# Five gate panels in seven half-size products each, with the gates kept in DRAM

## The chip, the core and the metric

The kernel runs on one core of a Trainium2 chip. The metric is the device time of one launch, in microseconds; lower is better. Matmuls run on TensorE (PE), element-wise work on VectorE (DVE) and ScalarE (ACT), and transfers are issued from the queues of SyncE (SP) and GpSimd (POOL).

## The reference, cut to what matters

One decoder layer over 1024 prompt tokens and 64 sample tokens, which the kernel handles together as TOK = 1088 columns. D_MODEL is 1024. The part that the change touches is this:

```python
u = rmsnorm(x)
a, q, k, v, g_a, g_b = split(u @ w_in)          # g_a and g_b are 1024 wide each
A = pooled(a) @ w_pa                            # 512 -> 1024
B = attention(q, k, v) @ w_pb                   # 256 -> 1024
h = x + (sigmoid(g_a) * A + sigmoid(g_b) * B) @ w_o
y = h + relu(rmsnorm(h) @ w_up)**2 @ w_down
```

## The kernel before, in words

Activations lie transposed in SBUF, features on the 128 partitions and the 1088 tokens along the free axis: `act[0][k]` and `act[1][k]` are the high and low part of feature block k (0 to 7). Every fp32 operand is split in two this way (`split`: ACT copies the high part, DVE subtracts it to get the low part), and every product takes three passes (high by high, high by low, low by high). A gemm over 8 feature blocks is thus 24 matmuls.

A weight panel is 1024 features by 256 outputs. `panel` loads it in pieces of 512 columns through a ring of three 256 KB buffers, tag `raw`, and splits each piece into one of three `places`. A raw buffer takes its next load only when ACT and DVE have both read it. Other things go through the same ring, among them the operands of the mix.

The order on PE is the order in which the code is written (a manual schedule). The order on the other engines and queues comes from the framework's scheduler; each engine then runs its own list strictly in turn.

The stages around the change, in order of time:

- Gates: eight panels, ga0 to ga3 and gb0 to gb3. `gate` computes one unit: one of three token chunks (384, 384, 320) by one of two output blocks m, 24 matmuls into one PSUM bank (`pga`, `pgb`), then a multiply on DVE with the norm `rb_g` and a sigmoid on ACT. The first two panels run among the last of the attention work.
- Mix: `branches` loads the pooled and the attention features through the raw ring and splits them into `ab`. For each panel d and unit, `pa` is 12 matmuls and `pb` 6; DVE multiplies them with the gates and adds. For d below 3 the result is split and stored to DRAM (`mix_d`), and brought back into `act` at the end by POOL transfers. Mix units alternate with units of gb on PE.
- w_o: four panels d, chunk by chunk, m = 0 then m = 1, each gemm into a bank of its own out of four (`acc_tile`, tile name `ph`). DVE adds the residual `xr` on the way out into `y` (line 1161).
- Up and down projections, with a scheme of seven half-size products (M1 to M7). Such a product is 24 matmuls of 272 columns into a `pair`, a PSUM tile of two banks, and `unit` runs the seven of them. `prep_up` forms and splits the sums of weight quarters.

## Time and profile before

| | us |
|---|---|
| median of 3 runs | 1484.96 (1481.98 to 1486.16) |
| profiled execution | 1481.76, of which the span of the trace is 1480.0 |
| PE busy | 1445.0 (98%) |
| DVE busy | 1011.0 (68%) |
| ACT busy | 686.6 (46%) |
| POOL busy | 411.3 (28%) |

Times within the trace are counted from the start of the span. The granted clock of PE averages 0.989 of full speed. In the stretches that the change touches, gates begin at 408.7 us, the mix ends at 681.98, w_o runs from there, and the first up product begins at 781.07.

### The profile page before, as it was taken

How to read it: one execution, taken by the hardware profiler on the slowest of the kernel's cores; microseconds unless marked ns; L12 is line 12 of the kernel's file. 1: busy time of each engine (PE TensorE's matmuls, PEld its weight loads, DVE VectorE, ACT ScalarE, POOL GpSimd, SP SyncE). 2: the span in 40 equal slices, each digit the busy share in tenths (PEclk: the TensorE clock that was granted, in tenths of full speed). 3: DMA queues.
4: the chain of work that ended last, by engine and by line, in shares of the span. 5: the costliest groups of instructions: out<-in, count | busy, mean ns of one | idle time of the engine just before them, and what ended most of it. 6: DMA issues, size and time to landing. Idle time of an engine off the chain costs nothing.

```text
span 1480.0 us, 28012 instructions
## 1 busy us (share of the span) xinstructions
PE 1445.0 (98%) x10595; PEld 1396.9 (94%) x10595; DVE 1011.0 (68%) x1949; ACT 686.6 (46%) x1885; POOL 411.3 (28%) x619
## 2 busy tenths in 40 slices
PE   8999899999999999999998999999999999999998
PEld 8988788878999999999998999999998999999998
DVE  7555555767864443434668989888987566777786
ACT  8566755567774222222345665655555322222220
POOL 1611246645400000010200121111225444544430
PEclk9999999999999999999999999999999999999999
DMA  6311766874445657478620767766768797567542
GB/s 218 97 47 63 194 144 169 210 185 116 125 140 178 221 167 255 163 205 285 249 101 25 288 263 265 277 249 250 258 256 312 294 365 305 228 269 279 218 186 113
DMA packets 124277, 304.72 MB, mean 206 GB/s; under 512 B 19111, under 2 KB 72045, under 8 KB 118830
## 3 DMA queue, kind: packets, MB, share of 16 engines
q1 hardware_dynamic: 102334, 192.27, 39.4%
q0 software_dynamic: 21376, 109.88, 20.4%
q8 instruction: 83, 1.36, 0.4%
q10 hardware_dynamic: 432, 0.79, 0.2%
q14 instruction: 52, 0.43, 0.1%
HBM read 218.49 MB, written 128.05 MB: 234 GB/s over the span
## 4 chain that ended last, share of the span: by engine, by line
PE 75%; issue 11%; DMA 5%; DVE 4%; POOL 3%; ACT 1%; SPq 0%; POOLq 0%; ACTq 0%; DVEq 0%
PE p1d L1199 12%; PE pga L136 6%; PE pgb L136 6%; PE ph L136 6%; PE pqk L136 6%; PE p2d L1199 6%; PE p1u L1199 5%; PE pv L136 4%; PE a L264 3%; PE pa L136 3%; PE p3d L1199 3%; PE p2u L1199 2%; POOL z_d L1332 2%; DMA raw_qkv<-in_w_in_dram 2%; DVE places L94 2%
## 5 line engine op out<-in xcount | busy, mean ns | idle before, releaser
L1199 PE MATMUL p1d<-act,places 128*128 128x272 f32 x1104 | 191.3, 288 | 3.2 <-DVE yd L1579 1.4
L1199 PEld LDWEIGHTS p1d<-act,places 128*128 128x128 f32 x1104 | 163.1, 188 | 4.7 <-DVE yd L1579 2.5
L1332 POOL DMA_DIRECT2D z_d<-zs_M x105 | 56.2, 536 | 244.4 <-DVE zs_M L94 241.2
L1629 POOL DMA_DIRECT2D out_kv_sample_dram<-in_cache_kv_dram x44 | 22.1, 504 | 318.4 <-ACT places L93 302.0
L1199 PE MATMUL p1u<-act,places 128*128 128x272 f32 x768 | 104.5, 293 | 5.2 <-DVE y L1161 3.9
L1579 DVE TENSOR_TENSOR yd<-yd,p1d 128x544 f32<-128x544 f32 x116 | 83.0, 716 | 38.6 <-PE p1d L1199 38.4
L1199 PEld LDWEIGHTS p1u<-act,places 128*128 128x128 f32 x768 | 100.9, 193 | 5.8 <-ACT act L1285 4.1
L93 ACT ACTIVATE places<-sd 128x512 fp32r<-128x512 f32 x64 | 37.4, 625 | 143.7 <-issue 106.9
L1199 PE MATMUL p1u<-t,places 128*128 128x272 f32 x768 | 101.5, 288 | 0.7 <-ACT q L1446 0.7
L1199 PEld LDWEIGHTS p1u<-t,places 128*128 128x128 f32 x768 | 98.2, 188 | 0.8 <-ACT q L1446 0.8
L136 PE MATMUL pga<-act,places 128*128 128x384 f32 (+1 forms) x576 | 98.0, 328 | 0.0
L136 PE MATMUL pgb<-act,places 128*128 128x384 f32 (+1 forms) x576 | 97.8, 326 | 0.0
L1199 PE MATMUL p2d<-act,places 128*128 128x272 f32 x528 | 94.0, 288 | 1.7 <-DVE places L94 1.0
L136 PEld LDWEIGHTS pgb<-act,places 128*128 128x128 f32 x576 | 95.4, 188 | 0.0
L136 PE MATMUL ph<-act,places 128*128 128x384 f32 (+2 forms) x624 | 95.4, 314 | 0.0
L136 PEld LDWEIGHTS ph<-act,places 128*128 128x128 f32 x624 | 95.3, 188 | 0.0
L136 PEld LDWEIGHTS pga<-act,places 128*128 128x128 f32 x576 | 94.6, 188 | 0.3
L93 ACT ACTIVATE places<-rd 128x512 fp32r<-128x512 f32 x64 | 37.1, 625 | 94.6 <-PE p1d L1199 94.6
L1199 PEld LDWEIGHTS p2d<-act,places 128*128 128x128 f32 x528 | 78.8, 188 | 2.3 <-DVE places L94 1.2
L561 POOL TENSOR_TENSOR mr<-ms,mhalf 128x4 f32<-128x4 f32 (+2 forms) x39 | 49.8, 1276 | 110.6 <-DVE ms L560 105.0
L1531 POOL TENSOR_TENSOR sd<-rd 128x128 f32<-128x128 f32 x64 | 38.5, 602 | 128.9 <-DVE places L94 115.0
L94 DVE TENSOR_TENSOR zs_M<-q,zs_M 128x544 fp32r<-128x544 f32 x75 | 54.0, 722 | 19.1 <-ACT zs_M L93 19.0
(383 smaller groups left out, 3674.0 us busy)
## 6 DMA issues: line engine op xcount, KB each, us to landing
z_d<-zs_M POOLq DMA_DIRECT2D x105, 544.0 KB, 4.6
act<-z_d SPq DMA_DIRECT2D x73, 544.0 KB
out_kv_sample_dram<-in_cache_kv_dram POOLq DMA_DIRECT2D x36, 960.0 KB, 7.4
ru<-in_w_up_dram SPq DMA_DIRECT2D x16, 1024.0 KB
rd<-in_w_down_dram SPq DMA_DIRECT2D x15, 1024.0 KB
raw_qkv<-in_w_in_dram SPq DMA_DIRECT2D x36, 256.0 KB
zc<-z_d SPq DMA_DIRECT2D x16, 544.0 KB
pck<-in_cache_kv_dram SPq DMA_DIRECT2D x32, 256.0 KB
```

The costliest lines, as they stand in the source:

```text
L93: ins = s_.activation(dst_hi, src, AF.Copy)
L94: v_.tensor_tensor(dst_lo, src, dst_hi.bitcast(F32), op=ALU.subtract)
L136: last_mm[0] = t_.matmul(out, lhs(a, k), rhs(b, k), start=(j == 0), stop=(j == len(terms) - 1))
L264: last_mm[0] = t_.matmul(pts[m][:, :n], wt[:, a, kk, m * P:(m + 1) * P], act4[b][kk][:, :, part4(c)], start=(p == 0 and kk == 0), stop=(p ...
L561: g_.tensor_tensor(r[:n, :H], ms[:n, :H], mhalf[:n, :H], op=ALU.pow)
L1199: last_mm[0] = t_.matmul(pt[:, s, :R4], w(a, k), z(b, k, s), start=(start and j == 0), stop=(j == len(terms) - 1), skip_group_check=True)
L1332: g_.dma_start(z_d[f][AT[m]], st.rearrange("p b l -> p (b l)").bitcast(F32))
L1531: ins = g_.tensor_tensor(s[:, 0], a21, a22, op=ALU.add)
L1579: v_.tensor_tensor(part, part, p[src], op=ALU.add)
L1629: ins = g_.dma_start(d, a)
```

## The change

Panels ga0 and ga1 stay as they are, and ga2 is done plainly too, but in four quarters of 272 tokens, the later half of the tokens first. The other five (ga3, gb0 to gb3) become units g0 to g4 of seven products each. For them the quarters of the token matrix are formed anew from the input `xT`, read again in eight loads through one buffer `xg`, scaled by ACT, added on DVE and split into `gt` (the sums) and into the second half of `act`. All gates go to DRAM (`g_d`) and come back in the mix, one feature block kk at a time. The mix starts after all gates, in 16 halves of `pa` (24 matmuls of 272) and `pb` (12), and its result is split straight into `act`; `mix_d` is gone. `ab` is now six tiles in the memory that `gt` had. In w_o both m of a chunk share one `pair` tile instead of a bank each. The diff, cut:

```diff
-    for d in range(4):
-        sga = (sga0, sga1)[d] if d < 2 else [gate("a", d, c, m, wga, 12) for c, m in units]
...
-            gemm(pa_[:, :n], 4, lambda s, k: wab[:, s, k, ms], lambda s, k: ab[:, s, k, cs])
...
-                split(st[:, 0, :n], st[:, 1, :n], ga[:, :n])
-                dma_st(mix_d[c][:, :, 2 * d + m, :n], st[:, :, :n].bitcast(F32))
...
+    for d in range(3):
+        for u, (c0, n) in enumerate([(r * R4, R4) for r in (2, 3, 0, 1)] if d == 2 else CHUNKS):
...
+    weight_sets(("g", 0), raw_u[0], ORDER_G[0], GBASE, 0)
+    for k in range(4):
+        def quarters_of(n):
+            x = gc.tile([P, TOK], F32, name=f"xg{k}{n}", tag="xg", bufs=1)
+            dma(x, i["xT"][:, k + 4 * n])
...
+            for h in (1, 0):
+                s_.activation(by_half(ts[h]), x.rearrange("p (l r) -> p r l", r=4)[:, 2 * h:2 * h + 2],
+                              AF.Copy, scale=ln1[:, k + 4 * n:k + 4 * n + 1])
+            return ts
+        b11, b12 = quarters_of(0)
+        b21, b22 = quarters_of(1)
...
+        split(gt[0][k][:, 0], gt[0][k][:, 1], b12)
...
+        split(act[0][k][:, h1], act[1][k][:, h1], b21)
...
+            if m == "M1":
+                q["11"] = part("q11", 1)
+                s_.copy(q["11"], p1)
...
+            g_.dma_start(g_d[x][2 * d + m][:, (h0, h1)[h]], t.rearrange("p s l -> p (s l)"))
...
+    for n in range(NU):
+        if n:
+            weight_sets(("g", n), raw_u[0], ORDER_G[n], GBASE, n)
+        unit(f"g{n}", 4, lambda m, a, k, n=n: sets_of[("g", n), m][:, a, k], gate_z, gate_done(n, n == 0), ORDER_G[n],
+             whole=n == NU - 1, apart=n == 0)
...
+    ab = [abp.tile([P, 2, TOK], F32R, name=f"ab{k}") for k in range(6)]
+    for k in range(6):
+        src = (amix_d[:, k] if k < 4 else attn_d[:, k - 4]).rearrange("p q l -> p (q l)")
+        for c0, n in ((0, 512), (512, 512), (1024, 64)):
+            raw = temp(f"b{k}_{c0}")[:, :n]
+            dma(raw, src[:, c0:c0 + n])
+            split(ab[k][:, 0, c0:c0 + n], ab[k][:, 1, c0:c0 + n], raw)
+    for kk in range(KD):
+        d, m = divmod(kk, 2)
+        if m == 0:
+            wab = by_k(panel(i["w_ab"][d], f"ab{d}"))
+        gs = [rr(gx, [P, TOK], F32, name=f"g{x}{kk}", tag=f"g{x}", bufs=2) for x in "ab"]
+        for x in range(2):
+            dma(gs[x], g_d[x][kk])
...
+                pt = pair(2 * h + x, f"p{'ab'[x]}{kk}_{h}")
+                product(pt, k1 - k0, ...)
+            split(act[0][kk][:, hs], act[1][kk][:, hs], gs[0][:, hs])
...
         for c0, n in CHUNKS if d < 3 else [(r * R4, R4) for r in range(4)]:
+            pt = pair((2, 0, 3, 1)[(c0 // R4 if d == 3 else 3 * d + c0 // CH) % 4], f"ph{d}_{c0}")
             for m in range(2):
                 kk = 2 * d + m
-                po = acc_tile(f"ph{kk}_{c0}")
+                po = pt[:, m]
```

Three places in the order of the instructions show where things stand now. Names end in a buffer number.

First, ACT at the entry to the units, in the kernel after. `b30`, `b31` are the scaled halves of the last two `xg` loads, `gt2_3` and `gt3_3` the last sums, `places` are weight sets, and the COPY takes the first product M1 of unit g0 out of PSUM.

```order
L1148 ACTIVATE b301_6454<-xg30_6451,cols_59 128x544
L1148 ACTIVATE b300_6453<-xg30_6451,cols_59 128x544
L93 ACTIVATE places_68<-rg1_6480 128x512
L93 ACTIVATE gt1_3_6345<-b301_6454 128x544
L93 ACTIVATE places_68<-s('g', 1)_M5_6651 128x512
L1148 ACTIVATE b311_6460<-xg31_6457,cols_59 128x544
L1148 ACTIVATE b310_6459<-xg31_6457,cols_59 128x544
L1159 ACTIVATE gt2_3_6349<-t2f3_6463 128x544
L93 ACTIVATE places_68<-s('g', 1)_M6_6655 128x512
L93 ACTIVATE gt3_3_6353<-b300_6453 128x544
L93 ACTIVATE act0_63<-b310_6459 128x544
L93 ACTIVATE places_68<-rg1_6480 128x512
```

The next row after these is the COPY `gq11_0_6507<-p1g0_6482`: it stands behind the whole chain of `xg` loads. Before, nothing of this was there.

Second, SP's queue at the entry to the mix, after: `b4`, `b5` are the raw pieces of the attention features, `ga`, `gb` the gates that come back, `raw_ab0` the first panel of the mix's weights.

```order
L1244 DMA b3_0_7594<-amix_d_74 128x512
L1252 DMA ga0_7642<-g_da0_5429 128x1088
L1244 DMA b3_512_7598<-amix_d_74 128x512
L1244 DMA b3_1024_7602<-amix_d_74 128x64
L1252 DMA gb0_7643<-g_db0_5437 128x1088
L1252 DMA ga1_7732<-g_da1_5430 128x1088
L1244 DMA b4_0_7606<-attn_d_75 128x512
L1252 DMA gb1_7733<-g_db1_5438 128x1088
L1244 DMA b4_512_7610<-attn_d_75 128x512
```

And ACT's list at the same place, from the last sigmoid of the gates (`gq21_4`) on:

```order
L1178 ACTIVATE gq21_4_7539<-gq21_4_7539 128x544
L93 ACTIVATE ab2_7551<-b2_0_7582 128x512
L93 ACTIVATE ab2_7551<-b2_512_7586 128x512
L93 ACTIVATE ab2_7551<-b2_1024_7590 128x64
L93 ACTIVATE ab3_7552<-b3_0_7594 128x512
L93 ACTIVATE ab3_7552<-b3_512_7598 128x512
L93 ACTIVATE ab3_7552<-b3_1024_7602 128x64
L93 ACTIVATE ab4_7553<-b4_0_7606 128x512
L93 ACTIVATE ab4_7553<-b4_512_7610 128x512
L93 ACTIVATE ab4_7553<-b4_1024_7614 128x64
```

Then come the three rows of `ab5` and the three of `raw_ab0`. Two thirds of the mix's operands and all its weights now stand behind the last sigmoid, while before they were split among the gates' matmuls.

Third, PE in w_o with what each row waits for, before:

```order
L136 MATMUL ph2_384_8320<-act0_63,places_68 128x384 [waits DVE_49,PE_49]
L136 MATMUL ph2_384_8320<-act0_63,places_68 128x384 x7
L136 MATMUL ph2_384_8320<-act1_64,places_68 128x384 x8
L136 MATMUL ph2_384_8320<-act0_63,places_68 128x384 x8
L136 MATMUL ph3_384_8349<-act0_63,places_68 128x384 [waits DVE_49,PE_49]
```

and after:

```order
L136 MATMUL ph1_384_8809<-act0_63,places_68 128x384 [waits PE_49]
L136 MATMUL ph1_384_8809<-act0_63,places_68 128x384 x7
L136 MATMUL ph1_384_8809<-act1_64,places_68 128x384 x8
L136 MATMUL ph1_384_8809<-act0_63,places_68 128x384 x8
L136 MATMUL ph1_384_8809<-act0_63,places_68 128x384 [waits DVE_49]
```

Before, a gemm waited for DVE to have emptied the bank that was used four gemms earlier. After, the last row, the m = 1 gemm, waits for DVE to have taken the m = 0 gemm just ahead of it out of the same `pair`.

More of the change, by code (lines that the diff above doesn't have):

```diff
@@ L1037, in early @@
-    def early(x, d, wt, n):
-        ts = []
-        for c, m in units[n]:
-            ts.append(gate(x, d, c, m, wt, 12 if x == "a" else 3))
-            if ab is None and not active and not waiting:
-                branches()
-        return ts
-    abp = psc = None
-    wga = by_k(panel(i["w_in"][11], "ga0"))
-    sga0 = early("a", 0, wga, slice(0, 2))
-    wga1 = by_k(panel(i["w_in"][12], "ga1", after=marks[1:2] * 4))
-    sga0 += early("a", 0, wga, slice(2, 5))
-    wgb = by_k(panel(i["w_in"][15], "gb0", after=marks[4:5] * 4))
@@ new lines, in decoder_step, with gate @@
+    g_d = [[dp.tile([P, TOK], F32, name=f"g_d{x}{kk}") for kk in range(KD)] for x in "ab"]
+    pg1, pg2, pt_ = ExitStack(), ExitStack(), ExitStack()
+    gp = pg1.enter_context(tc.tile_pool(name="gates", bufs=1, side="right", reuse_waits="tile"))
+    rb_g = gp.tile([P, TOK], F32, name="rb_g")
+    dma(rb_g, bass.AP(tensor=r_d.tensor, offset=r_d.offset, ap=[[0, P], [1, TOK]]))
+    gc = pg2.enter_context(tc.tile_pool(name="plain", bufs=1, side="right", reuse_waits="tile"))
+    def gate(d, c0, n, m, wt):
+        pg = acc_tile(f"pga{d}_{c0}_{m}")
+        gemm(pg[:, :n], KD, lambda s, k: wt[:, s, k, m * P:(m + 1) * P], lambda s, k: act[s][k][:, c0:c0 + n],
+             middle=step)
+        t = rr(gc, [P, CH], F32, name=f"sga{d}_{c0}_{m}", tag="sga", bufs=2)
+        v_.tensor_tensor(t[:, :n], pg[:, :n], rb_g[:, c0:c0 + n], op=ALU.mult)
+        s_.activation(t[:, :n], t[:, :n], AF.Sigmoid)
+        dma_st(g_d[0][2 * d + m][:, c0:c0 + n], t[:, :n])
+        marks.append(last_mm[0])
+        step()
@@ new lines, in decoder_step @@
+    marks = [last_mm[0]]
+    wga = [by_k(panel(i["w_in"][11], "ga0"))]
+    for d in range(3):
+        for u, (c0, n) in enumerate([(r * R4, R4) for r in (2, 3, 0, 1)] if d == 2 else CHUNKS):
+            if d < 2 and u == 1:
+                wga.append(by_k(panel(i["w_in"][12 + d], f"ga{d + 1}", after=marks[1:2] * 4)))
+            for m in range(2):
+                gate(d, c0, n, m, wga[d])
+    while active or waiting:
+        step()
+    flush()
+    pb2.close()
+    pb.close()
+    pacc.close()
@@ new lines, in decoder_step, with cell_s, load_gate @@
+    cds = pool("raws", reuse_waits="tile")
+    def cell_s(tag, shape, dt, name):
+        return cds.tile(shape, dt, name=name, tag=tag, bufs=1)
+    pp = ctx.enter_context(tc.tile_pool(name="pairs", bufs=1, space=PSUM, reuse_waits="tile"))
+    for n in (3, 1, 2, 0):
+        pair(n, f"first{n}")
+    raw_u = [None]
+    def load_gate(n):
+        raw_u[0] = cell_s("d", [P, KD, 2 * P], F32, f"rg{n}")
+        dma(raw_u[0], i["w_in"][14 + n].rearrange("p (k n) -> p k n", k=KD))
+    NU = 5
+    GBASE = 8
```

342 lines of the change are left out of this document (175 added, 167 removed).

## The prediction

> **What bounds the kernel now.** I read the busy shares first, then the stretches of time that the change touches, then the chain of work that ended last, then the idle times of PE, and last the queues of ACT and DVE at the places that get a new wait. Busy shares, and busy time by stretch (time, PE, PEld, DVE, ACT, POOL, granted clock, DMA share, GB/s):
>
> ```profile
> PE 1445.0 (98%) x10595; PEld 1396.9 (94%) x10595; DVE 1011.0 (68%) x1949; ACT 686.6 (46%) x1885; POOL 411.3 (28%) x619
> ...
> 500.00:612.00 112.00, 112.00 (x685) 112.00 (x684) 50.41 (x97) 29.00 (x56) 4.83 (x10) 1.00 0.53 179
> 612.00:682.00 70.00, 70.00 (x431) 70.00 (x430) 28.91 (x55) 16.15 (x31) 7.88 (x12) 1.00 0.77 225
> 682.00:777.00 95.00, 95.00 (x624) 94.95 (x623) 56.21 (x101) 35.16 (x61) 11.82 (x13) 1.00 0.59 215
> 777.00:781.00 4.00, 0.17 (x2) 0.00 (x0) 4.00 (x9) 4.00 (x9) 0.00 (x0) 0.82 0.18 70
> 781.00:838.00 57.00, 55.01 (x408) 53.68 (x408) 49.95 (x83) 32.53 (x59) 7.11 (x11) 0.95 0.38 138
> ```
>
> PE is busy in every microsecond of gates, mix and w_o, at full clock. So PE's work there is time one for one, and so is any wait that the change puts in front of PE. The one idle stretch, 777 to 781, is at the start of the up stage. PE's idle times there, in brackets:
>
> ```profile
> 759.81 17.36 PE L136 MATMUL ph<-act,places 128*128 128x272 f32 x137
> 781.07 5.63 PE L1199 MATMUL p1u<-act,places 128*128 128x272 f32 x24 [3.90 <-DVE y L1161]
> 786.54 3.15 PE L1199 MATMUL p2u<-act,places 128*128 128x272 f32 x24
> ...
> 801.31 3.28 PE L1199 MATMUL p1u<-t,places 128*128 128x272 f32 x24 [0.70 <-ACT q L1446]
> ...
> 838.61 3.27 PE L1199 MATMUL p1u<-act,places 128*128 128x272 f32 x24 [1.27 <-ACT q L1374]
> ```
>
> An idle time of 3.90 us made the next 24 matmuls take 5.63 instead of 3.0, which is 2.6 us more; 0.70 and 1.27 us cost nothing beyond themselves.
>
> **PE's work, saved.** From the chain that ended last (start, duration, what):
>
> ```profile
> 449.12 19.54 PE pga L136 x120
> ...
> 487.40 4.16 PE pgb L136 x24
> ...
> 494.68 3.51 PE pgb L136 x24
> ...
> 551.62 23.70 PE pga L136 x144
> ...
> 681.98 93.97 PE ph L136 x614
> ...
> 786.70 2.99 PE p2u L1199 x24
> 789.69 3.02 PE p3u L1199 x24
> ```
>
> A plain panel is 144 matmuls in 23.70 us; a half-size product is 24 matmuls in 3.005 (mean of the last two rows), so a unit of seven takes 21.03. Five of them save 5 x 2.67 = 13.3. ga2 in quarters is 8 x 3.005 = 24.04, which costs 0.3. The mix was 18 matmuls a unit: 18/24 of 4.16 for the 16 units of 384 columns and of 3.51 for the 8 of 320, 71.0 in all. It becomes 16 x 36 matmuls of 272, 24 x 3.005 = 72.1, 1.1 more. Net: -11.9 us. Nothing hides it, so it comes in full. w_o, up and down issue the same matmuls.
>
> By these rows the plain gates (ga0 and ga1 end at 449.12 + 19.54 = 468.66, as now) would end at 492.7.
>
> **Entry to the units.** The token quarters pass one at a time through one buffer `xg`: load 544 KB, two ACT copies, next load. The last reads of the old data must come first: ACT's write to the second half of `act` for k = 0 waits for ga2's second quarter, which ends near 480.6, and ACT runs its list in turn. From there five loads follow each other. The trace has no load of that size with a landing time; the nearest row is the store of 544 KB, 4.6 us, and I take it (lower bound 3, upper bound 7, from the larger transfers below):
>
> ```profile
> z_d<-zs_M POOLq DMA_DIRECT2D x105, 544.0 KB, 4.6
> ...
> act<-mix_d POOLq DMA_DIRECT2D x4, 1152.0 KB, 9.4
> ...
> rd<-in_w_down_dram POOLq DMA_DIRECT2D x1, 1024.0 KB, 6.9
> ```
>
> ```profile
> L94 DVE TENSOR_TENSOR zs_M<-q,zs_M 128x544 fp32r<-128x544 f32 x36 | 25.7, 718 | 7.1 <-ACT zs_M L93 7.1
> L93 ACT ACTIVATE zs_M<-q 128x544 fp32r<-128x544 f32 x36 | 23.5, 656 | 4.0 <-DMA z_d<-zs_M 2.4 <-DVE q L1344 0.7
> ...
> L1374 ACT COPY q<-p1u 128x544 f32<-128x544 f32 x8 | 4.8, 601 | 0.2 <-PE p1u L1199 0.2
> ```
>
> With 1.3 us for two copies of 544 columns (656 ns each) a link of the chain is 5.9 us, and five end at 480.6 + 29.5 = 510.1. The copy of M1 (`gq11_0`) stands behind this on ACT, and product M6, fifth of the unit, waits for that copy because it adds into the same PSUM pair. M6 starts at 510.7; without the wait it would start at 492.7 + 4 x 3.0 = 504.7. That is 6.0. Behind it come 1.2 where M7 waits for ACT's copy of M6 (0.60 in the row, and signals), 1.2 where g1's first product waits for a DVE sum that stands behind the late load `rg2` (1 MB, the 6.9 row), and 0.3 of signals: **+8.6**, from 3 (landing 3.1 us, the chain just met) to 15 (7 us).
>
> [...]
>
> **Entry to the mix.** `ab` lies where `gt` was and its pieces go through the three raw buffers, as do the weights `raw_ab0` behind them. What a turn of that ring takes is in ACT's list of before:
>
> ```profile
> 453.65 1.67 ACT L93 ACTIVATE ab<-raw_b 128x512 fp32r<-128x512 f32 x3 [3.60 <-DMA attn_d<-atg0b]
> ...
> 457.93 0.63 ACT L93 ACTIVATE ab<-raw_b 128x512 fp32r<-128x512 f32 x1 [1.83 <-DMA raw_b<-amix_d]
> ...
> 462.02 0.63 ACT L93 ACTIVATE ab<-raw_b 128x512 fp32r<-128x512 f32 x1 [0.87 <-DMA raw_b<-amix_d]
> ...
> 465.72 0.63 ACT L93 ACTIVATE ab<-raw_b 128x512 fp32r<-128x512 f32 x1 [1.45 <-DMA raw_b<-amix_d]
> ...
> 469.76 0.63 ACT L93 ACTIVATE ab<-raw_b 128x512 fp32r<-128x512 f32 x1 [1.42 <-DMA raw_b<-attn_d]
> ...
> 473.90 0.63 ACT L93 ACTIVATE places<-raw_ab 128x512 fp32r<-128x512 f32 x1 [2.16 <-DMA raw_ab<-in_w_ab_dram]
> ```
>
> Five turns from 453.65 to 473.90, 4.05 us each. There they ran under gate matmuls. After the change, ACT's list puts ab2 to ab5 and the weights behind the last sigmoid. Let U be the start of the last unit; its eight products (the owed one of the unit before among them) end at U + 24, and the last sigmoid, after a DVE multiply and itself 0.65, at U + 25.7. ab2's three pieces have landed by then. Four more turns bring the weights: 25.7 + 16.2 = 41.9, and 1.3 till the third piece. In SP's queue `ga0` and `ga1` stand ahead of pieces of ab3 and ab4, and wait until the gates' buffers are stored (4.6 us after the sigmoid); they and the 2.2 MB that they and `gb0`, `gb1` move add 2 to 3. PE, done at U + 24, begins `pa0` near U + 45: **+21**, from 17 (four turns alone) to 27 (turns of 5.5 us beside those loads). An idle time of that length is followed by the half clock of the row at 781.07: **+2.6**.
>
> **w_o.** The m = 1 gemm of each chunk now waits for DVE to have emptied the m = 0 half of the same pair, which DVE can only begin when that gemm has ended. What DVE needs for it:
>
> ```profile
> 694.36 1.72 DVE L1161 TENSOR_TENSOR y<-ph,xr 128x272 f32<-128x272 f32 x4 [6.18 <-DMA xr<-in_xT_dram]
> ...
> 697.21 0.88 DVE L1161 TENSOR_TENSOR y<-ph,xr 128x160 f32<-128x160 f32 x2
> ...
> 703.52 0.78 DVE L1161 TENSOR_TENSOR y<-ph,xr 128x48 f32<-128x48 f32 x2
> ...
> 780.28 0.64 DVE L1161 TENSOR_TENSOR y<-ph,xr 128x272 f32<-128x272 f32 x1
> ```
>
> About 0.85 for the two pieces of a half (0.88, 0.78 in the rows), and 0.35 for two signals (from DVE to PE 781.07 - 780.92 = 0.15; 0.2 the other way is an estimate): 1.2 us in each of nine chunks, 10.7. In the last panel, in quarters, it is 0.64 + 0.35 four times, and DVE there is 3 to 5 us behind with splits for the up stage; on the other hand the wait of 3.90 at 781 shrinks, as PE's pauses let DVE catch up. I take +4.2 (between 0, if the shorter wait at 781 and its 2.6 of half clock pay for it, and 8). The first half also waits for `xr0`: before, DVE got it only at 694.36, 12.4 us after w_o began, and PE had three more banks to go on with; now it stops after one gemm of 4.2. The load may be issued earlier, with POOL's copies of `mix_d` gone from the channel, so I take +3 (0 to 8). Sum: **+17.9**, from 9 to 25.
>
> Steady units, the mix itself (DVE 6.9 us a block by 0.72 an operation, PE 9.0) and the stores of `g_d` lie under PE's work; if DVE's 0.72 grew by a third, the mix would be bound by it.
>
> **Sum.** 1481.8 - 11.9 + 8.6 + 21 + 2.6 + 17.9 = **1520.0**. That is against the profiled execution; the median of the runs before is 3.2 higher, and I add 1 for it: **1521**. Low ends together 1499, high ends 1540.
>
> **Rivals.**
>
> 1. Cover, the other side: ACT and DVE, idle 54% and 32% of the time, run so far ahead that PE finds every wait met. Then only PE's work counts: 1481.8 - 11.9 = 1470, and up to 1475 with small gaps. It decides once all waits together are under 12 us. For it: before, the same raw ring was wholly covered. Against: in w_o DVE can't begin before the gemm that PE has just done, nine times 1.2 alone being 10.7. Chance 0.05.
> 2. The mix's operands come in time, because the scheduler's order on ACT turns out not to hold the early pieces back and the queue's loads overlap; the rest stays: 1520 - 21 - 2.6 = 1496. Against: three buffers and 15 pieces behind the sigmoid. Chance 0.15.
> 3. Loads land later than priced, at all three places, since stores of gates, `xg`, `rg`, `ab` and gates reloaded share the channel (0.77 of it busy at 612 to 682 already): links of 7 us, turns of 5.5, `xr0` 8 us: 1540. Chance 0.17.
> 4. Clock: the repeated pauses of w_o halve the clock each time. Price by the row at 781.07: 13 x 2.6 = 34 more, 1554. Against: 0.70 and 1.27 were followed by 3.28 and 3.27. Chance 0.03. [...]
>
> The forecast itself has 0.60. The range 1491 to 1541 holds rivals 2 and 3 and leaves out 1 and 4 and the tails of both. A measurement of this kernel tells about 0.3% (4.5 us) from no change: faster 0.05 (rival 1), same 0.03 (rival 2 with w_o at its low end), slower 0.92.
>
> **What would show it.** In the trace after, PE has seven products of 3.0 us a unit and 105 us of them; an idle time of 4 to 8 us before the fifth product of g0, released by ACT; one of 17 to 27 before the first `pa`, released by ACT's `places` or `ab`, with the next 24 matmuls near 5.6; and thirteen of about 1 us in w_o, released by DVE's `y`. The prediction is wrong if the idle time before `pa` is under 10, or if w_o takes less than 103 us from its first to its last gemm.

## The result, and the profile after

The changed kernel takes 1554.60 us (median of 6 runs, 1548.88 to 1568.74) against 1483.66 us (1481.98 to 1486.16) for the kernel before: ratio 1.049, 95% interval 1.0439 to 1.0540. It is slower, as forecast, but by 71 us where 36 were forecast, and the time lies outside the range of 1491 to 1541. The profiled execution took 1551.04 us, its span is 1549.2, which is 69.2 more than before.

First the busy shares, and then busy time by stretch of the kernel after (time, PE, PEld, DVE, ACT, POOL, granted clock, DMA share, GB/s). The stretches are: end of attention and plain gates; first unit; the other units; entry to the mix and the mix; w_o.

```profile
PE 1451.9 (94%) x10907; PEld 1396.6 (90%) x10907; DVE 1059.0 (68%) x1996; ACT 731.0 (47%) x1935; POOL 416.1 (27%) x633
```

```profile
408.00:507.00 99.00, 90.35 (x614) 88.17 (x613) 52.90 (x146) 60.07 (x121) 4.16 (x7) 0.95 0.55 178
507.00:539.00 32.00, 23.31 (x146) 22.55 (x146) 19.52 (x31) 18.02 (x27) 0.58 (x1) 0.79 0.35 107
539.00:627.00 88.00, 87.72 (x700) 87.50 (x698) 43.78 (x69) 33.82 (x58) 12.85 (x24) 1.00 0.48 170
627.00:728.00 101.00, 76.00 (x576) 75.27 (x576) 59.67 (x94) 27.77 (x49) 6.36 (x13) 0.86 0.85 295
728.00:851.00 123.00, 102.32 (x625) 98.35 (x626) 60.89 (x110) 39.22 (x67) 10.67 (x11) 0.97 0.35 129
```

PE's column holds two losses at once. Time minus busy time is waiting. Busy time above what the work took before is, for the most part, slow clock, which means that matmuls ran at a reduced rate (the granted clock of the first unit is 0.79): before, w_o was 95.17 busy (95.00 + 0.17 in the prediction's rows), here it is 102.32 for the same 624 matmuls. Only the steady units (539 to 627) show neither loss: 29 products in 87.3 us, 3.01 each, as forecast.

Before, the end of attention with its gates had neither loss either. The same view of the kernel before:

```profile
408.00:481.00 73.00, 73.00 (x491) 72.02 (x490) 41.64 (x126) 44.96 (x93) 2.25 (x5) 1.00 0.52 157
```

From PE's timeline of the kernel after, its longest waits in these stretches and the rows that are read below:

```profile
424.57 0.66 PE L616 MATMUL tpg0b<-ident,smg0b 128*128 128x128 f32 x4 [3.27 <-ACT ocg0b L631]
450.26 0.66 PE L720 MATMUL tcg0b<-ident,ocg0b 128*128 128x128 f32 x2 [3.49 <-DVE ocg0b L654]
450.58 12.27 PE L136 MATMUL pga<-act,places 128*128 128x320 f32 x60
507.20 3.19 PE L1014 MATMUL p1g<-act,places 128*128 128x272 f32 x24
521.98 5.13 PE L1014 MATMUL p2g<-gt,places 128*128 128x272 f32 x21 [5.18 <-ACT gt L93]
529.86 5.50 PE L1014 MATMUL p1g<-gt,places 128*128 128x272 f32 x24 [2.75 <-ACT gq L1187]
536.12 3.29 PE L1014 MATMUL p1g<-gt,places 128*128 128x272 f32 x24 [0.76 <-ACT gq L1196]
539.24 3.17 PE L1014 MATMUL p1g<-act,places 128*128 128x272 f32 x24
649.88 0.82 PE L1014 MATMUL pa<-ab,places 128*128 128x272 f32 x2 [23.16 <-ACT places L93]
651.85 5.36 PE L1014 MATMUL pa<-ab,places 128*128 128x272 f32 x22 [1.15 <-ACT places L93]
730.32 4.43 PE L136 MATMUL ph<-act,places 128*128 128x384 f32 x24 [2.62 <-DVE ga L1260]
735.72 8.60 PE L136 MATMUL ph<-act,places 128*128 128x384 f32 x48 [0.98 <-DVE y L1324]
791.64 8.62 PE L136 MATMUL ph<-act,places 128*128 128x384 f32 x48 [2.02 <-DVE y L1324]
838.09 7.78 PE L136 MATMUL ph<-act,places 128*128 128x272 f32 x48 [2.70 <-DVE y L1324]
850.88 3.26 PE L1014 MATMUL p1u<-act,places 128*128 128x272 f32 x24 [1.06 <-DVE y L1324]
```

And the row of the kernel before that answers to the 60 matmuls at 450.58:

```profile
439.20 9.70 PE L136 MATMUL pga<-act,places 128*128 128x320 f32 x60
```

Three things were forecast and stand here: a wait of 4 to 8 us in the first unit (in two pieces: 5.18 inside the fourth product, for `gt`, which was not forecast, and 2.75 ahead of the fifth, for ACT's copy of M1, where all of it was), the wait of 17 to 27 us for ACT's `places` ahead of the first `pa` (23.16 + 1.15), and waits for DVE's `y` in w_o (14 of them, 17.3 us in all). Two were not. The attention's own small matmuls (`tpg0b`, `tcg0b`) now wait for ACT and DVE, where PE had no wait at all before, and the first unit begins at 507.20 instead of 492.7. And the slow clock follows far more of the waits than one: the 60 matmuls of 320 and 384 columns took 12.27 where they took 9.70 before; products took 5.13 (21 of the 24 matmuls), 5.50 and 5.36 (22 of 24); 48 matmuls of 272 took 7.78, where the same group at 818.78, without slow clock, took 6.31.

The account closes. Waiting is time minus busy in the stretch; the rest is busy time minus the work at the prediction's rates (84.7 for the first stretch, which is 492.7 - 408; 18.0 for six products; 72.1 for the mix; 95.2 for w_o).

| stretch | waiting: forecast | measured | busy beyond the work (slow clock): forecast | measured |
|---|---|---|---|---|
| attention's end, plain gates | 0 | 8.7 | 0 | 5.7 |
| first unit | 8.6 | 8.7 | 0 | 5.3 |
| entry to mix, mix | 21 | 25.0 | 2.6 | 3.9 |
| w_o and its end, less 3.8 of before | 17.9 | 16.9 | 0 | 7.1 |
| sum | 47.5 | 59.3 | 2.6 | 22.0 |

59.3 + 22.0 - 11.9 of saved work = 69.4, against 69.8 at the first up product and 69.2 in the spans. The 22.0 are a remainder. The rows that ran slow account for some 15 of it, each measured against a row of the same size without slow clock: 4.5, 4.7, 3.2 and 3.0 by stretch. The rest is small change, 0.1 to 0.3 us in each row that stands behind a wait, and 0.5 by which the first stretch began late.

### The profile page after: what moved, and what is told of

Its sections match the earlier page's. It is cut to its first block, busy times and chain, and to the rows that moved or that the text cites. A ratio compares the mean times of both kernels' runs of the same rounds, so it can differ in the third digit from the quotient of the medians.

```text
span 1549.2 us, 28823 instructions
## 1 busy us (share of the span) xinstructions
PE 1451.9 (94%) x10907; PEld 1396.6 (90%) x10907; DVE 1059.0 (68%) x1996; ACT 731.0 (47%) x1935; POOL 416.1 (27%) x633
## 4 chain that ended last, share of the span: by engine, by line
PE 29%; issue 12%; DVE 4%; POOL 2%; DMA 2%; ACT 1%; POOLq 0%; ACTq 0%; DVEq 0%
PE p1d L1014 11%; PE p2d L1014 5%; PE ph L136 4%; PE p1u L1014 3%; PE p3d L1014 2%; POOL z_d L1411 2%; PE p2u L1014 2%; DVE places L94 1%; DMA z_d<-zs_M 1%; DVE yd L1658 1%; PE p3u L1014 1%; DVE y L1324 1%; DMA ru<-in_w_up_dram 0%; DVE act L94 0%; DMA rd<-in_w_down_dram 0%
## 5 line engine op out<-in xcount | busy, mean ns | idle before, releaser
L136 PE MATMUL ph<-act,places 128*128 128x384 f32 (+2 forms) x624 | 102.2, 324 | 19.9 <-DVE y L1324 17.3
L136 PE MATMUL pga<-act,places 128*128 128x384 f32 (+2 forms) x480 | 78.5, 324 | 1.4 <-ACT qk L566 1.0
L1014 PE MATMUL pa<-ab,places 128*128 128x272 f32 x384 | 53.9, 298 | 25.0 <-ACT places L93 24.3
L136 PEld LDWEIGHTS pga<-act,places 128*128 128x128 f32 x480 | 75.0, 197 | 2.2 <-ACT qk L566 1.3
L1014 PEld LDWEIGHTS pa<-ab,places 128*128 128x128 f32 x384 | 51.7, 197 | 25.7 <-ACT places L93 24.8
```

The costliest lines, as they stand in the source:

```text
L136: last_mm[0] = t_.matmul(out, lhs(a, k), rhs(b, k), start=(j == 0), stop=(j == len(terms) - 1))
L1014: last_mm[0] = t_.matmul(pt[:, s, :R4], w(a, k), z(b, k, s), start=(start and j == 0), stop=(j == len(terms) - 1), skip_group_check=True)
```

## Experiments

Ratios are to the kernel before, run on the same chip; "the kernel after" is the changed kernel. A trace is one execution. The six runs of the kernel after lie 20 us apart, and in the traces of the five kernels that share the code up to there (after, own_pairs, ring6, need, fill) the first unit begins anywhere between 505.99 and 513.19. Differences smaller than that show nothing by themselves.

### w_o: a pair of banks for each gemm (own_pairs)

```diff
-            pt = pair((2, 0, 3, 1)[(c0 // R4 if d == 3 else 3 * d + c0 // CH) % 4], f"ph{d}_{c0}")
...
-                po = pt[:, m]
+                turns["ph"] = turns.get("ph", -1) + 1
+                po = pair((2, 0, 3, 1)[turns["ph"] % 4], f"ph{kk}_{c0}")[:, 0]
```

> Edit: in w_o each gemm gets a pair of its own, in turn out of four, instead of both m of a chunk sharing one. Theory: the thirteen waits for DVE's y in w_o (18.5 us of idle time in the trace, and 3.5 of half clock after the two of 2.46 and 2.70) come from the shared tile alone. They go, apart from one wait of about 4 us before the up stage as in the kernel before with its 2.6 of half clock: w_o and the start of up take 99 to 104 us instead of 123, total 1529 to 1535. Rival: DVE is late by itself there (it runs the evacuations, the splits for up and the squares), so the waits move to the next bank and the stage stays above 115, total 1541 to 1549.

Measured: 1533.68 us, ratio 1.0341 (1.0315 to 1.0366), 20.9 under the kernel after. PE's timeline of this run, all of w_o in one row:

```profile
735.62 95.34 PE L136 MATMUL ph<-act,places 128*128 128x384 f32 x624
830.79 3.19 PE L1014 MATMUL p1u<-act,places 128*128 128x272 f32 x24
```

All waits for `y` are gone, and with them the slow clock; even the wait of 3.90 that the kernel before had ahead of up is gone. The pair shared by both m was the whole cost of w_o, in waits and in clock. From the first gemm of w_o to the first up product are 95.2 us instead of 120.6; that the whole kernel gained only 20.9 fits a first unit that began 6 us later in this trace (513.19), in a part that the edit doesn't touch.

### The mix's operands: more buffers, another order, and work in the gap (ring6, need, fill)

Ring6 lets the `ab` pieces alternate between the three raw buffers and three of their own. Need keeps three buffers and loads the pieces in the order in which the first products use them. Fill puts 200 matmuls, whose result nobody reads, into PE's gap ahead of the mix.

```diff
 ring6
-            raw = temp(f"b{k}_{c0}")[:, :n]
+            if c0 % 1024 if k % 2 else not c0 % 1024:
+                raw = rr(abp, [P, 512], F32, name=f"b{k}_{c0}", tag="rawb", bufs=3)[:, :n]
+            else:
+                raw = temp(f"b{k}_{c0}")[:, :n]
 need
-    for k in range(6):
+    for j, (k, c0, n) in enumerate([(k, c0, 512) for ks in ((0, 1, 2, 3), (4, 5)) for c0 in (0, 512) for k in ks] +
+                                   [(k, 1024, 64) for k in range(6)]):
...
 fill
+    idle = pair(3, "idle")
+    for j in range(200):
+        t_.matmul(idle[:, j % 2, :240], act[0][7][:, :P], act[0][7][:, :240], start=True, stop=True, ...)
```

> Edit: the 18 raw pieces of ab alternate between the three raw buffers and three more of their own; the weights stay on the three. Theory: the idle time of 24.3 us at the entry to the mix is the throughput of the ring, 21 pieces through three buffers at about 4 us a turn. With six buffers the pieces cost two engine operations of 0.65 to 0.7 each: the idle time falls to 10 to 15 us, total 1536 to 1542. Rival: the order on ACT, in which two thirds of the pieces stand behind the last sigmoid of the gates, or the gate loads that wait for stores, set it; then it stays above 20, total 1545 to 1551.

> Edit, alone: the pieces of ab are loaded in the order in which the mix reads them (first both 512-column pieces of tiles 0 to 3, then of 4 and 5, the six 64-column pieces last), through the same three buffers. Theory: the wait at the entry to the mix is the number of turns of the ring ahead of the first weights, which stay last; 21 pieces are 21 pieces, so it stays at 20 to 25 us, total within 4 us of the changed kernel (1546 to 1553). Rival: the 64-column pieces, each a turn with a transfer of its own, hold up the others; then 4 to 8 us go.

> Edit, alone: 200 matmuls of 240 columns on data that nobody reads fill the idle time before the first product of the mix (some 22.5 of 24.3 us). The mix does not start earlier for it. Theory: the first 24 matmuls of pa took 5.4 us in place of 3.0, and 12 of pb 2.0 in place of 1.5, because the clock was halved after the idle time. With PE kept busy they run at 3.0 to 3.3 and 1.7, the entry to the mix costs 2.5 to 3 us less. Rival: they are slow because weights and ab arrive piece by piece; then their durations stay.

Measured: ring6 1538.54, ratio 1.0370 (1.0354 to 1.0385), 16 under the kernel after; need 1555.12, 1.0475 (1.0460 to 1.0490), no gain; fill 1546.35, 1.0424 (1.0393 to 1.0455). PE's rows ahead of the first `pa`, of ring6, of need and of fill:

```profile
638.60 0.82 PE L1014 MATMUL pa<-ab,places 128*128 128x272 f32 x2 [10.73 <-ACT places L93]
641.26 5.20 PE L1014 MATMUL pa<-ab,places 128*128 128x272 f32 x22 [1.85 <-ACT places L93]
```

```profile
650.14 5.61 PE L1014 MATMUL pa<-ab,places 128*128 128x272 f32 x24 [23.05 <-ACT places L93]
```

```profile
624.53 22.57 PE L1248 MATMUL idle<-act 128*128 128x240 f32 x200
648.66 0.52 PE L1014 MATMUL pa<-ab,places 128*128 128x272 f32 x2 [1.56 <-ACT places L93]
650.73 4.56 PE L1014 MATMUL pa<-ab,places 128*128 128x272 f32 x22 [1.55 <-ACT places L93]
```

With twice the buffers the wait falls from 24.3 to 12.6; in another order through three buffers it stays at 23. So the number of turns of the ring sets it, not which piece comes first. Fill left two short waits, and the product behind them still took 4.56 for 22 matmuls: from the first `pa` to the second are 7.97 us, against 8.95 in the kernel after. It tested the clock and answered only half: a filled gap brings back 1.0 us, and behind the waits of 1.56 and 1.55 the matmuls ran slow again. That fill's median lies 8 us under the kernel after is more than this 1.0 and isn't explained by it.

### Attention's end (hold_copies, hold_sets, late_ga2, late_hold)

In the kernel after, ACT's and DVE's lists hold work of the new units among the last attention work. From ACT's list (the copies of `xg`, and attention's `ocg0b` behind them), DVE's list, and POOL's queue:

```profile
412.77 2.55 ACT L1148 ACTIVATE b<-xg,cols 128x544 f32<-128x544 f32 x2
421.88 2.38 ACT L1148 ACTIVATE b<-xg,cols 128x544 f32<-128x544 f32 x2
424.17 0.35 ACT L631 COPY ocg0b<-pog0b 128x256 f32<-128x256 f32 x1
```

```profile
448.49 1.29 DVE L1065 TENSOR_TENSOR s('g', 0)_M<-rg 128x512 f32<-128x512 f32 x2 [2.40 <-DMA rg<-in_w_in_dram]
449.70 0.42 DVE L654 TENSOR_TENSOR ocg0b<-ocg0b,olg0b 128x256 f32<-128x256 f32 x1
```

```profile
433.18 1.22 POOL L1708 DMA_DIRECT2D out_kv_sample_dram<-in_cache_kv_dram  x2 [22.50 <-ACT places L93]
```

ACT's `ocg0b`, for which PE waited 3.27 us, comes right behind two copies; DVE's, for which it waited 3.49, right behind a weight sum that waited for a load. POOL's two copies of 960 KB follow the splits of panel ga2 and start at 433.18, where before they started at 441.75: the loads of ga2 are held to an earlier point than those of the third panel before. Each was taken away alone, then all three.

```diff
 hold_copies: the first two copies of xT wait for ga0's last matmul
+                ins = s_.activation(...)
+                if k == 0 and n == 0:
+                    behind_pe(ins, marks[6])
 hold_sets: so do g0's weight sums and their first split
-    weight_sets(("g", 0), raw_u[0], ORDER_G[0], GBASE, 0)
+    weight_sets(("g", 0), raw_u[0], ORDER_G[0], GBASE, 0, marks[6])
... (inside weight_sets, behind_pe with this mark on the sums and the first split)
 late_ga2: ga2's pieces are loaded from ga0's fourth gate on
-... after=marks[1:2] * 4)))
+... after=(marks[4:5] if d else marks[1:2]) * 4)))
 late_hold: all three
```

> Edit: the scaled copies of the first xT load (and so all that follow) wait for the last matmul of panel ga0; nothing else is changed. Theory A: the 14.5 us by which the plain gates ended late (507.2 instead of 492.7) come from unit preparation that the scheduler put among the attention's own steps, on ACT (four strided copies, 4.9 us by 412.8 and 421.9) and on DVE (a weight sum that waits for rg0). Then this kernel loses the idle time of 3.27 us before the transposes (released by ACT's ocg0b) and its half clock, but not the one of 3.49 behind the weight sum: the plain gates end about 6 to 8 us earlier. The entry to the units (14.0 us late) stays or grows by a few us, since the chain of xT loads starts later; total 1541 to 1549. Rival C: the late end comes from transfers that share the channel with the attention's (xT, rg0); then the gates end within 3 us of before, total 1548 to 1553.

> Edit: the weight sums of unit g0 and its first split wait for the last matmul of panel ga0; the load rg0 and the xT copies stay where they are. Theory A: the idle time of 3.49 us (DVE's ocg0b stands behind a sum that waits 2.4 us for rg0) goes, with the half clock after it (60 matmuls in 12.27 us instead of 8.8): the plain gates end 5 to 7 us earlier, total 1543 to 1547. Rival C, transfers: rg0's 1 MB load is still there at the same place, so the olg0b landing and the end of the gates stay, total 1548 to 1553.

> Edit: the pieces of panel ga2 wait for the fourth gate of ga0 (as those of the third panel, gb0, did in the kernel before) instead of the first. Theory D: the late end of the plain gates comes from transfers. The third panel of weights is split 9 us earlier than before, and POOL's cache copies (two of 960 KB), which are tied to the splits of that panel, start at 433 instead of 442, in the middle of the attention's last loads (olg0b landed 5 us after the wait for it began, against 2.5). Then the first unit starts 5 to 9 us earlier than 507.2, total 1540 to 1547. Rival A, unit preparation in the lists of ACT and DVE alone: no change in the start of the units beyond 2 us, total 1548 to 1553.

> Edit: panel ga2 held as above, and also the copies of xT and the weight sums of unit g0 held until the last matmul of ga0. If the tail of the attention is disturbed by both (lists and transfers), only this kernel gets it back whole: the first unit starts at 493 to 496, 11 to 14 us earlier, total 1536 to 1543, with the entry to the units at 14 to 17 us as before. If the stores of the gates and the xT loads on SP's queue do it, the start stays after 500.

| | median us | ratio (95%) | first unit product at |
|---|---|---|---|
| kernel after | 1554.60 | 1.0490 (1.0439 to 1.0540) | 507.20 |
| hold_copies | 1551.97 | 1.0477 (1.0447 to 1.0507) | 508.99 |
| hold_sets | 1550.92 | 1.0466 (1.0439 to 1.0494) | 505.45 |
| late_ga2 | 1549.31 | 1.0449 (1.0416 to 1.0483) | 503.14 |
| late_hold | 1543.17 | 1.0406 (1.0391 to 1.0422) | 494.69 |

PE's longest waits for `ocg0b`, of hold_copies and then of late_hold, with late_hold's first unit product:

```profile
448.21 0.41 PE L720 MATMUL tcg0b<-ident,ocg0b 128*128 128x128 f32 x2 [3.01 <-DVE ocg0b L654]
461.96 0.66 PE L720 MATMUL tcg0b<-ident,ocg0b 128*128 128x128 f32 x2 [3.91 <-DVE ocg0b L654]
```

```profile
450.36 0.41 PE L720 MATMUL tcg0b<-ident,ocg0b 128*128 128x128 f32 x2 [1.32 <-DVE ocg0b L654]
494.69 3.19 PE L1014 MATMUL p1g<-act,places 128*128 128x272 f32 x24
```

Together the edits moved the first unit by 12.5 of the 14.5 us, far outside the spread of untouched traces, and the six joined kernels further down, which hold all three, start it at 493.92 to 497.80. Alone, none of them met its forecast: the moves, from 1.8 us later to 4.1 earlier, hardly leave the spread of 505.99 to 513.19, and no ratio lies outside the interval of the kernel after. By their own signs hold_copies and hold_sets spoke for transfers and against the lists. The profiled execution of hold_copies, at 1560.98 us, was also its slowest. But the waits that each edit was aimed at did change. With the copies held, the wait of 3.27 for ACT's `ocg0b` shrank to 0.20, and PE waited 3.01 and 3.91 for DVE's instead. With the sums held, the one of 3.49 for DVE's was gone, and 3.87 for ACT's `ocg0b` and 2.31 for another tile of ACT's stood there. With ga2 held, 4.46 for ACT's `ocg0b` stayed and DVE's longest was 1.45. Where one obstacle was gone, the work came late by another; by any one of these runs a real cause would have been cleared. How much of it is order in the lists, and how much the transfers that the same edits move, these runs don't separate.

### The first unit's chain (halves, m7)

Halves loads xT in two half loads with two buffers, so that a load can run beside the copies. M7 gives g0's M7 weight sum a raw buffer; in the kernel after it takes the single buffer `s`, which `t2f` of the token quarters takes too.

```diff
 halves
-            x = gc.tile([P, TOK], F32, name=f"xg{k}{n}", tag="xg", bufs=1)
-            dma(x, i["xT"][:, k + 4 * n])
+            x = [rr(gc, [P, H], F32, name=f"xg{k}{n}{j}", tag="xg", bufs=2) for j in range(2)]
+            for j in range(2):
+                dma(x[j], i["xT"][:, k + 4 * n, j * H:(j + 1) * H])
... (ACT's copies, now two for each half load)
 m7
-... (cell_s("s", [P, H], F32, name)[:, :512] if m == "M7" else temp(name)) ...
+... (cell_s("s", [P, H], F32, name)[:, :512] if m == "M7" and key != ("g", 0) else temp(name)) ...
```

> Edit: each xT row block is loaded in two halves through two buffers of half the size, so that one half lands while ACT copies the other. Theory: the waits of unit g0 (5.2 and 2.8 us idle before M5 and M6, and 2.5 us of half clock after each) come from the chain of five loads and five pairs of strided copies (6.5 us a link: 4.0 load, 2.45 copies). With halves a link is about 4: the waits before M5 and M6 go or fall under 2 us in all, and 8 to 12 us with them: from the first product of g0 to the first of g1 20 to 23 us instead of 32, total 1539 to 1545. Rival: the chain is set by its start (ACT's write to act after ga2's second quarter) and by the other work on ACT's list; then less than 4 us are gained.

> Edit, alone: the weight sum for M7 of unit g0 goes into a raw buffer instead of the small buffer s, which it shares with the token sums t2f. Theory: the start of the chain of xT loads is set by neither the loads nor the write to act. The M7 sum holds the buffer s until its split, the split waits for a slot of places that panel ga1 reads until its last gate (480.6 in the changed kernel's trace), so the first token sum t2f, and in ACT's list the copies of the third xT load that landed at 430, stand behind it until 484. With the buffer free the chain runs under ga1: from the first product of g0 to the first of g1 18 to 22 us instead of 32, total 1538 to 1546. Rival: the write to act after ga2's second quarter holds the chain anyway (two buffers for b21); then 27 or more stay and the total is 1547 or more.

ACT's list in the kernel after, at the head of the chain and two of its later links:

```profile
480.59 1.22 ACT L93 ACTIVATE places<-s('g', 0)_M 128x512 fp32r<-128x512 f32 x2 [0.41 <-PE pga L136]
...
484.78 1.30 ACT L1148 ACTIVATE b<-xg,cols 128x544 f32<-128x544 f32 x1
...
511.63 2.46 ACT L1148 ACTIVATE b<-xg,cols 128x544 f32<-128x544 f32 x2 [2.61 <-DMA xg<-in_xT_dram]
...
518.08 2.40 ACT L1148 ACTIVATE b<-xg,cols 128x544 f32<-128x544 f32 x2 [2.01 <-DMA xg<-in_xT_dram]
```

And in m7:

```profile
468.94 2.43 ACT L1148 ACTIVATE b<-xg,cols 128x544 f32<-128x544 f32 x2
475.42 2.46 ACT L1148 ACTIVATE b<-xg,cols 128x544 f32<-128x544 f32 x2 [2.60 <-DMA xg<-in_xT_dram]
482.16 2.43 ACT L1148 ACTIVATE b<-xg,cols 128x544 f32<-128x544 f32 x2 [2.77 <-DMA xg<-in_xT_dram]
```

Measured: halves 1557.06, ratio 1.0504 (1.0484 to 1.0525), from the first unit's start to the second's 29.4 us against 32.0; m7 1549.09, 1.0450 (1.0425 to 1.0475), 26.6 us against 32.0. A link is 6.05 to 6.74 us, of which two copies are some 2.45 and the load 3.65 to 4.3 (the lowest of both is the last link of the kernel after, 518.08 to 524.13). Halves shortens the waits in the fourth and ahead of the fifth product (3.36 and 1.61 instead of 5.18 and 2.75) and hardly the entry. M7 starts the chain some 15 us earlier, and the waits in the fourth and ahead of the fifth product are gone, though a new one of 5.45 for a gate's multiply on DVE, with slow clock behind it (5.09 for 24 matmuls at 515.74), stands ahead of the second product. So the entry is 5.4 us shorter where up to 14 were to be had, and the time of the whole kernel doesn't show it beyond the intervals. Both runs missed what was expected of them. What started the chain late was a split of `s`, which waited for `places` that ga1 read to its last gate, with the token work in the same buffer behind it.

### All together (all_late, h1, h1_gs, all_m7_gs, all_need, all_g2)

Now the edits are joined. The question is whether the saved work of 11.9 us shows once the new waits are gone. All_late joins own_pairs, ring6, halves, late_hold and the mix's first weights loaded during the last unit. H1 adds loads of xT from ACT's queue and plain gates that read the later half of the tokens first; h1_gs also reloads the gates from ACT's queue. All_m7_gs is all_late with m7, with the splits of M6, M7 and M4 of g0 held to ga2's second quarter, and with the gates reloaded from ACT's queue. All_need adds the order of need for `ab`. All_g2 also holds g2's weight sums behind g1's first product.

```diff
 all_late, early mix weights
+        if n == NU - 1:
+            place[0] = 19
+            wab = by_k(panel(i["w_ab"][0], "ab0"))
...
-        if m == 0:
+        if m == 0 and d:
 h1 (the order of the plain gates isn't shown), h1_gs
-                dma(x[j], i["xT"][:, k + 4 * n, j * H:(j + 1) * H])
+                s_.dma_start(x[j], i["xT"][:, k + 4 * n, j * H:(j + 1) * H])
...
-            dma(gs[x], g_d[x][kk])
+            s_.dma_start(gs[x], g_d[x][kk])
 all_m7_gs, the held splits
-            if mark is not None and m == order[0]:
-                behind_pe(ins, mark)
+            if mark is not None and m in (order[0], "M6", "M7", "M4"):
+                behind_pe(ins, mark if m == order[0] else marks[16])
 all_g2
-            weight_sets(("g", n), raw_u[0], ORDER_G[n], GBASE, n)
+            weight_sets(("g", n), raw_u[0], ORDER_G[n], GBASE, n, ends["g1", "M1"] if n == 2 else None)
... (in unit: ends[name, m] is the product's last matmul)
```

> Edit: all together: pairs of their own in w_o, six buffers for ab, the first weights of the mix loaded before unit g4, xT in halves, unit preparation held until ga0's end, ga2 held. By the ledger of the traces: 1481.8, less 11.9 of PE's work, and what is left of the waits: attention's tail 1 to 4, entry to the units 2 to 6, entry to the mix 6 to 13 with its half clock, mix to w_o 1 to 3, start of up 0 to 2. Sum 1480 to 1498. Below 1479 it would beat the kernel before. If the waits only move to the next bound (DVE, the channel), it stays above 1505.

> Edit, on top of all the edits together: the xT loads are issued from ACT's queue instead of SP's (there they stand behind gate stores that wait for sigmoids), and the plain gates that read the later half of the tokens run first, ga1's first chunk and ga2's first two quarters last, so that act may be written 8 us earlier. Theory: with all edits the entry to the units still costs 11 us (29.4 from the first product of g0 to the first of g1, 18 needed), because the chain of xT loads is paced by SP's queue and by the write to act after ga2's second quarter. Then the entry falls to 18 to 24 us and the total to 1485 to 1491. Rival: ACT's own list (copies, weight splits, sigmoids) is the pace; then 27 or more stay, total 1493 to 1499.

> Edit, on top of the one before: the gates come back in the mix through ACT's queue instead of SP's. Theory: with all edits the mix takes 85.8 us for 72.1 of matmuls, and its waits are released by DVE's multiply, which waits for gates that stand in SP's queue behind weight pieces (raw_ab, raw_o) that wait for a raw buffer. Then the mix takes 73 to 79 us and the total falls by 6 to 11 against the run beside it; at 1479 or less it beats the kernel before. Rival: two buffers for each gate are too few whichever queue issues the loads (a turn is load 4 to 5 us, multiply, add and split of both halves, against 9 us of PE a block); then the mix stays above 81.

> Edit: all together as before (pairs of their own in w_o, six buffers for ab, first mix weights early, xT in halves, preparation and ga2 held), with the M7 sum of g0 in a raw buffer, its M6 and M7 splits held until ga2's second quarter, and the gates reloaded through ACT's queue. From 1495.9 without the last three: less 8 to 11 for the entry to the units (29.4 us, 18 needed) and less 2 to 4 for the mix (85.8 to 82): 1481 to 1486, level with the kernel before or a little faster. If the entry stays above 27 us, 1492 to 1496.

> Edit, on top of all_m7_gs: the pieces of ab in the order in which the mix reads them, through the six buffers. There the weights come early, so only the pieces are left: the first half of the mix needs twelve of them and not the six of 64 columns. Theory: its waits for ab (1.8, 0.3, 0.2 and 1.8 us, and about 4 of half clock) fall to under 2 in all, total 1481 to 1486: no difference from the kernel before that can be told, or a little faster. Rival: ACT and DVE (0.65 and 0.7 a piece, twelve pieces after the units' sums are read) are the pace; then less than 2 us are gained, 1487 to 1490.

> As all_need (level with the kernel before at 1484.7), and the weight sums of the third unit's gate panel are held behind the second unit's first product, so that VectorE's additions of the first unit's gates do not stand behind a sum that waits for the third panel's load. If that order is what makes the 2.85 us wait ahead of the second unit's fifth product and the half clock of about 1.6 us behind it, both go: about 1480 us, 0.997 of the kernel before. Rival: the third unit's splits then come late and make a wait of their own of 2 us or more ahead of its first product, and the time stays at 1483 to 1486 us.

| | median us | ratio (95%) | first unit, us | mix, us | w_o, us |
|---|---|---|---|---|---|
| all_late | 1495.90 | 1.0085 (1.0062 to 1.0108) | 29.2 | 87.4 | 95.3 |
| h1 | 1509.57 | 1.0175 (1.0147 to 1.0203) | 42.7 | 84.7 | 95.2 |
| h1_gs | 1511.66 | 1.0187 (1.0169 to 1.0206) | 43.1 | 82.4 | 95.3 |
| all_m7_gs | 1489.46 | 1.0044 (1.0026 to 1.0062) | 20.8 | 83.9 | 95.2 |
| all_need | 1484.72 | 1.0001 (0.9989 to 1.0013) | 20.9 | 79.6 | 95.3 |
| all_g2 | 1483.33 | 0.9993 (0.9982 to 1.0004) | 20.8 | 81.8 | 95.2 |

(First unit: from its first product to the second unit's first. Mix: from the first `pa` to the first `ph`. W_o: from there to the first up product.) All_late and all_need came out within what was expected of them, h1, h1_gs and all_m7_gs above it, and all_g2 at its rival's time.

H1 failed: the splits of g0's M6 and M7 sums stand in ACT's list ahead of the copies, and they wait for ga1's last gate, which h1 had moved behind half of ga2. ACT's row in h1, and PE's wait in the fourth product there:

```profile
483.08 1.33 ACT L93 ACTIVATE places<-s('g', 0)_M 128x512 fp32r<-128x512 f32 x2 [0.56 <-PE pga L136]
```

```profile
523.09 4.27 PE L1014 MATMUL p2g<-gt,places 128*128 128x272 f32 x21 [9.51 <-ACT gt L93]
```

That row led to all_m7_gs, where these splits are held to a later point and no longer stand ahead of the copies, and where M7's sum has its own buffer: with both the entry is 20.8. What each gives wasn't run apart. H1 and h1_gs together show that the gates' queue is worth 2 us to the mix, and no more.

PE's longest wait in the units of all_need, which stands ahead of g1's M5 (the second product of that unit's order, not the fifth, as the text ahead of the run has it), the longest in its mix, and then the two rows that answer to them in all_g2:

```profile
520.80 4.77 PE L1014 MATMUL p2g<-gt,places 128*128 128x272 f32 x24 [2.85 <-DVE gq L1191]
...
648.54 3.24 PE L1014 MATMUL pa<-ab,places 128*128 128x272 f32 x24 [2.78 <-DVE ga L1272]
```

```profile
518.27 3.19 PE L1014 MATMUL p2g<-gt,places 128*128 128x272 f32 x24
...
646.62 4.77 PE L1014 MATMUL pa<-ab,places 128*128 128x272 f32 x24 [4.66 <-DVE ga L1273]
```

In all_g2 the wait of 2.85 and the slow clock behind it went, and its mix began 4.1 us earlier (602.59 instead of 606.71). But there PE ran into a longer wait, 4.66 instead of 2.78, with slow clock behind it, and the two ratios, 1.0001 and 0.9993, can't be told apart. DVE's list names the reason:

```profile
645.15 0.69 DVE L94 TENSOR_TENSOR places<-raw_ab,places 128x512 fp32r<-128x512 f32 x1 [2.42 <-ACT places L93]
645.76 1.35 DVE L1273 TENSOR_TENSOR ga<-pa,ga 128x544 f32<-128x544 f32 x2
```

The multiply that empties `pa` stands behind a split of the next weights, which waits for ACT and that for a load. It is the same kind of wait once more; taking it away was not tried. So the best version stands level with the kernel before and doesn't beat it: its interval holds 1. In all_g2's profile the first unit begins 1.7 us later than the plain gates' work allows (494.43 against 492.7), waits from there to the end of the mix sum to 9.1 (1.46, 0.76, 1.46, 0.74 and 4.66), and 1.6 is slow clock: 12.4 together, about the 11.9 that the change saves.

## Why the prediction was wrong

The sign was right and the rivals that spoke for a gain were rightly small. The time was wrong by 34 us: between the profiled executions it is 31, of which the account above makes 12 unforeseen waiting and 19 unforeseen busy time. Rival 4's 1554 lies next to the measured 1554.60, but that is luck: it is made of 34 us of slow clock in w_o, where the rows show 3.0. By the steps:

- **PE's work, -11.9: right.** Units are 3.01 us a product and 87.3 for 29.
- **"ga0 and ga1 end at 468.66, as now": wrong, and this is the step that failed.** The plain gates were costed at what they took before, with the attention's end beside them unchanged, so the term was put at nothing. But the change put instructions of its own into the lists of ACT and DVE there and moved POOL's copies ahead, and PE's matmuls of attention waited: 8.7 of waiting and 5.7 of busy time beyond the work, 14.5 at the first unit product. The prediction looked at the queues of ACT and DVE where a new wait was meant, not where old work was passed. Late_hold shows that these three make most of it: with them taken out, the first product is at 494.69. Which of them, and by lists or by transfers, stays open.
- **The clock: mis-sized, some 15 in slow rows (22.0 with all busy time beyond the work) instead of 2.6.** It was charged once, behind the longest wait, and rows of 0.70 and 1.27 were read to mean that shorter waits are free. In the kernel after, waits of 0.98, 2.02 and 2.62 were free in w_o as well (8.60 and 8.62 for 48 matmuls of 384, 4.43 for 24), while 2.46, 2.70 and 2.75 were not (7.84 and 7.78 for 48 of 272 against 6.31, and 5.50 for 24). The rows of before that the prediction read had no wait between 1.27 and 3.90, so the term should have run from nothing to 2.6 for each wait in between. In own_pairs even 0.70 was not free (4.63 for the 24 matmuls behind it, last section). Rival 4 named the clock but charged it to all short pauses, at 0.03.
- **Entry to the units: the waiting right in size (8.7 for 8.6), by other parts, so in part by luck.** The chain of `xg` loads was right. But its first victim is the fourth product, which reads `gt` (5.18), and the wait of 1.2 ahead of g1's first product didn't come. The link is 6.5 instead of 5.9, since a copy that takes every fourth element lasts 1.27 us instead of 0.65, and the load 3.65 to 4.3 instead of 4.6. The start was not set by the write to `act` alone: m7 shows that the shared buffer `s` held it. The upper end of 15 also doesn't follow from its own landing time: links of 8.3 us end at 522.1, which makes 20.7.
- **Entry to the mix: right in kind, 25.0 for 21 (over the whole mix).** Ring6 confirms that it is the turns of three buffers, and need that the order of the pieces doesn't matter. Behind the last sigmoid (627.84 in ACT's list) came eight pieces of 512 columns and then the weights, 1.9 to 4.7 us apart, 23 us in all, where four turns of 4.05 were forecast.
- **w_o: right, waiting 16.9 for 17.9.** The single waits behind the first half of a pair are 0.72 to 1.20 where some 1.2 was taken, with 2.02, 2.46 and 2.70 among them, and own_pairs takes them all away. Of the 0.35 for two signals, the 0.2 from PE to DVE was an estimate that no run shows; where the m = 0 gemm ends at 744.32, DVE's two adds begin at 744.36 and take 0.88, and the m = 1 gemm begins at 745.29, which leaves 0.09 for both. At its start PE waited 2.62 us for the mix's last sum, and not for `xr`; that this meets the +3 is luck. The bounds of 9 and 25 don't follow from the parts either, which give 10.7 and 26.7.

The low side of the range assumed that costs could only fall away together; on the high side it had nothing for a stage that the change does not mean to touch. With its own parts added rightly the high side would have been 1547, still under the measured time.

## What to carry to other kernels

Where a scheduler orders engine lists, read the lists of the changed program for each old instruction that PE waits for, also ahead of the place of the change: what now stands in front of it, and on which load that in turn waits. When one of several such obstacles is taken away and nothing moves, take them away together before clearing any. And before counting saved matmuls, count the buffers of what remains: here 11.9 us of saved work came out level, and no better, once the shared pair, the ring and the shared sum had buffers of their own and the held instructions were out of the way.

## What the runs showed of the hardware

- **The clock.** The length of a wait didn't decide whether the matmuls behind it ran slow. In all_need a wait of 2.85 us was followed by 4.77 for 24 matmuls, instead of 3.19, and one of 2.78 in the same execution by 3.24 (its rows above). Across runs the two even change places: 0.70 ahead of a product of the up stage was followed by 4.63 in own_pairs (at 852.57) and by 3.28 in all_g2 (at 801.60), and these are rows of halves and of hold_copies:

```profile
533.81 4.81 PE L1014 MATMUL p1g<-gt,places 128*128 128x272 f32 x24 [1.83 <-ACT gq L1199]
```

```profile
697.41 3.24 PE L1014 MATMUL pa<-ab,places 128*128 128x272 f32 x24 [3.23 <-DVE ga L1262]
```

  So such a wait costs between nothing and about 2.6 us beyond itself (the most is 5.78 for 24 matmuls behind 2.97, in the mix of all_late), and no run here shows what decides it.
- **A read of every fourth fp32 element.** ACT's scaled copy of 544 such columns took 1.27 us (16 of them, 1238 to 1386 ns). Scaled copies of the same size that read densely, later in the same kernel, took 0.74:

```profile
L1148 ACT ACTIVATE b<-xg,cols x16: 1238/1272/1386, 412.8 to 525.3; 128x544 f32<-128x544 f32 x16
```

```profile
L1298 ACT ACTIVATE y<-y,cols 128x544 f32<-128x544 f32 x4 | 3.0, 741 | 1.7 <-DMA h_d<-y 1.7
```

  The factor is 1.7. The two groups read different tiles at different places of the kernel, and no run varied the stride alone, so that the stride makes the difference is not shown.
